# A decoder step on one core: other paces for the decode between two attentions, a query buffer of its own, and POOL loads put behind a norm

## The chip, the cores and the metric

The kernel runs on one core of a Trainium2 chip. The metric is the time of one execution on the device, in microseconds; for the kernel before it is 1862.74 us, the median of 3 runs (1859.68 to 1864.82). One more execution was profiled; all views of the profile come from it.

## What is computed

One step of a one-layer hybrid decoder, for a prompt of 1024 rows (model width 1024) and for 8 sample rows that share the weights. Cut to what matters here:

```python
# the prompt: 1024 rows
q, k, v, logf, u, z = mixer_inputs(rmsnorm(xp, g_mix), w_in, b_f, g_sgu_v)
xp = xp + merge_heads(fox_prompt(q, k, v, logf), sgu_prompt(u, z, w_s, b_s), g_att_out, g_sgu_out, w_o)
mk, mv = memory_kv(mem_prompt, g_mem, w_ck, w_cv)             # 256 memory rows
xp = xp + cross_attend(rmsnorm(xp, g_cross), mk, mv, w_cq, w_co)
xp = xp + conv_ffn(rmsnorm(xp, g_ffn), 0, w_up, conv_w, conv_b, w_down)
# the sample: 8 rows, each with 8192 cached positions in 64 pages
q, k, v, logf, u, z = mixer_inputs(rmsnorm(xs, g_mix), w_in, b_f, g_sgu_v)
att = fox_sample(q, k, v, logf, cache_k, cache_v, cache_logf, page_table)
xs = xs + merge_heads(att, sgu_sample(u, z, w_s, b_s), g_att_out, g_sgu_out, w_o)
xs = xs + cross_attend(rmsnorm(xs, g_cross), cache_mem_k, cache_mem_v, w_cq, w_co)
xs = xs + conv_ffn(rmsnorm(xs, g_ffn), state_conv, w_up, conv_w, conv_b, w_down)
```

`fox_prompt` is causal attention with 8 heads of 64 and a forget gate added to the scores; `fox_sample` is the same for one query row over the paged cache. Both groups are normed once more at the end. All data is float32.

## The kernel before

**Two streams.** `prompt()` and `sample()` are Python generators that emit instructions and yield now and then. The prompt's stream is the main one; the value that it yields is an estimate in microseconds of the TensorE work just emitted. The loop at the end of `build` (L1873 to L1894) adds this value to a credit `acc` and, while the credit has reached a whole pace, takes one advance of the sample's stream; an advance that yields w lowers the credit by w times the pace. After one main yield of t at most `int(t / pace) + 1` advances are taken. The pace is `PACE[phase]` (L76), so a smaller number means a denser sample stream. [...]

**The prompt's stages.** `p1` (L335) makes the input projection: columns for q, for the gates, for k, for v, and for z. Products of float32 data are split in a rounded high part and a rest, three matmuls each (L270 to L272, and L436 to L438 in `by_rows`, which does four blocks of rows at once). Before the last four blocks of z, at `tt == 4`, it calls `early()`, which takes one step of the first attention and one of the fill, and pauses the sample's stream until the first memory product has been emitted. Then come the first attention (rows 0 to 511) mixed one to one with the fill, which is the memory's key and value products (`pmem`, 8 steps of 5.2) and the gating of the first half (`gating`, 8 units); the second attention (rows 512 to 1023) alone; then for each half of the rows the merge, the output projection, the cross-attention (`cross`) and the gated MLP (`ffn`), and a last norm.

**One attention** (`attention`, L686) goes over four pairs of heads `hp`, two blocks of 256 rows each. `load` fetches a pair's rows of q (`qn`, L692), k and v through SyncE's queue. `setup` is a generator in two halves: the first transposes q (L710) and copies it to `qq` (L717 to L734), the second does the same for k (L739 to L752); between them it yields once. `scores` (L755) makes a block of scores (L767 to L771), takes the row maximum on VectorE (L773, or L776 in the second attention) and the exponential on ACT (L774, L777). `turn` transposes the result (L796) and copies it back (L801, L803), `values` multiplies with v (L812), `back` transposes the output (L832) and scales it (L834). Of each pair, eight score blocks yield 1.8 each; while the next pair is being set up, five more yields of 1 follow.

**Buffers.** `T2()` gives one of 7 rotating buffers of 128 x 520 float32, `U()` one of 18 of 4 KB per partition, `KV()` one of 4 of 8 KB per partition, `WRAW()` one of 4 for raw weights. A new use waits until the old one's readers are done. `ssq_into` (L225) takes the sum of squares on ACT and throws the squares into a buffer `junk`.

**The sample's stream.** `decode` (L1316): for each of the 8 rows 16 steps over the cached keys (`kstep`) and, later, 16 over the cached values (`vstep`, eight matmuls L1444 for two steps). `kstep` fetches 1 MB with an indirect DMA from POOL (L1368), then multiplies with q and sums, both on VectorE. In a phase whose name begins with "att" it does this in four pieces (L1375, L1376), each after a yield of 0.2, so that a step of five yields costs one pace; elsewhere in wider instructions (L1384, L1388). `sample_rest` (L1557) follows: output projection, norm, cross-attention, norm, MLP, with their weights and cached memory loaded through POOL's queue into `KV` buffers (L1548, L1607, L1609, L1646, L1700, L1745). Its products with one column block of weights are L284, L1653, L1709 and L1754. `rms8` (L1514) norms the 8 rows: two sums of squares on ACT, a sum and a scale on VectorE (L1520, L221), and the power -0.5 on POOL (L222); `sample_norm` then scales (L1528) and `sample_T` transposes (L309).

**The cross-attention's weights** (`weigh`, L1125): for two blocks of 128 rows at a time the scores (L1135), the negative row maximum on VectorE (L1137), its product with the rows' factor `rq`, on VectorE too (L1138), and the exponential on ACT with that product as bias (L1141).

## Time and profile before

| | |
|---|---|
| median of 3 runs | 1862.74 us |
| profiled execution | 1866.47 us |
| its span, first to last instruction | 1864.6 us |
| instructions | 24289 |
| mean granted TensorE clock | 0.98 |
| HBM traffic | 495.73 MB read, 23.93 MB written, 279 GB/s over the span |
| POOL's software DMA queue | 341.14 MB, 49.0% of 16 DMA engines |
| SyncE's and ACT's hardware DMA queues | 178.58 MB, 27.6% of 16 DMA engines |

How to read the views. PE is TensorE's matmul side and PEld its weight loads, DVE is VectorE, ACT ScalarE, POOL GpSimd, SP SyncE; SPq, POOLq and ACTq are the queues of an engine's sequencer. An instruction stands as line, engine, operation, out<-in by the program's tile names with buffer numbers left out, shapes, and a count. In a timeline the first two columns are the start and the time taken in us, and the brackets hold the idle time of the engine before it and what released it. A row of the waits gives the total in us, how often, and the longest. The slices are 40 equal parts of the span, 46.6 us each; a digit is the busy share in tenths.

### The profile page before, as it was taken

What the parts mean: (1) busy time and instruction counts of PE and PEld (TensorE: products, weight loads), DVE (VectorE), ACT (ScalarE), POOL (GpSimd) and SP (SyncE); (2) the same over time, 40 slices, a digit from 0 to 9 for tenths busy, and PEclk for the clock granted to TensorE, in tenths of its full rate; (3) what the DMA queues carried; (4) which work ended last, traced back from release to release, by engine and by line L of the source; (5) the groups of instructions that cost most, each with busy time, mean ns of one, the idle gap of its engine ahead of it and who ended that gap; (6) DMA issues with size and microseconds to landing.
All of it is one profiled execution on the core that took longest, in us unless ns stands there. A gap on an engine that the chain in (4) does not pass through costs nothing.

```text
span 1864.6 us, 24289 instructions
## 1 busy us (share of the span) xinstructions
PE 1787.5 (96%) x9239; PEld 1299.2 (70%) x9239; DVE 1398.8 (75%) x1736; ACT 735.8 (39%) x1341; POOL 499.3 (27%) x461
## 2 busy tenths in 40 slices
PE   8999999888998999999999999998999999999998
PEld 5887676556676667767777776766676668767765
DVE  4788667888778787989989899898874559644344
ACT  6332364466633535323333234234353333232332
POOL 1243323433142322223242223234322111101110
PEclk9999999899999999999999999999999999999999
DMA  8877886967687975878878789988869577767971
GB/s 316 290 267 265 312 276 239 298 231 230 238 345 287 346 289 209 309 249 328 304 279 319 260 305 344 355 311 329 304 241 349 203 291 259 264 205 260 356 263 59
DMA packets 157012, 521.27 MB, mean 280 GB/s; under 512 B 20808, under 2 KB 40520, under 8 KB 124128
## 3 DMA queue, kind: packets, MB, share of 16 engines
q0 software_dynamic: 57168, 341.14, 49.0%
q1 hardware_dynamic: 92816, 165.99, 25.8%
q10 hardware_dynamic: 6912, 12.59, 1.8%
q8 instruction: 73, 1.20, 0.3%
q14 instruction: 43, 0.35, 0.1%
HBM read 495.73 MB, written 23.93 MB: 279 GB/s over the span
## 4 chain that ended last, share of the span: by engine, by line
PE 59%; DMA 7%; DVE 5%; issue 4%; ACT 2%; POOL 1%; DVEq 0%; POOLq 0%; ACTq 0%
PE ba L270 8%; PE ba L272 8%; PE ba L271 8%; PE bb L270 4%; PE bb L271 4%; PE bb L272 4%; PE dv L1444 4%; DMA kv<-cache_v,kidx 2%; DMA kv<-cache_k,kidx 2%; DVE s L1388 1%; DVE kv L1384 1%; PE dv L1709 1%; PE ba L1021 1%; DMA u<-an_d 1%; PE bb L812 1%
## 5 line engine op out<-in xcount | busy, mean ns | idle before, releaser
L233 ACT ACTIVATE wh<-wr 128x1024 fp32r<-128x1024 f32 (+2 forms) x220 | 228.8, 1044 | 516.6 <-PE ba L271 192.0
L234 DVE TENSOR_TENSOR wl<-wr,wh 128x1024 fp32r<-128x1024 f32 (+2 forms) x220 | 262.9, 1201 | 144.6 <-PE ba L272 62.4
L1368 POOL DMA_INDIRECT kv<-cache_k,kidx x128 | 194.8, 1522 | 569.5 <-DVE s L1388 317.4
L1384 DVE TENSOR_TENSOR kv<-kv,d 128x1024 f32<-128x1024 f32 (+1 forms) x156 | 258.0, 1681 | 29.8 <-DMA kv<-cache_k,kidx 29.5
L1388 DVE TENSOR_REDUCE s<-kv 128x16 f32<-128x1024 f32 (+1 forms) x156 | 258.0, 1673 | 0.0
L1438 POOL DMA_INDIRECT kv<-cache_v,kidx x128 | 159.2, 1244 | 314.7 <-PE dv L1444 244.4
L270 PE MATMUL ba<-u,wh 128*128 128x512 f32 (+1 forms) x560 | 221.3, 397 | 2.0 <-ACT u L236 1.9
L271 PE MATMUL ba<-u,wh 128*128 128x512 f32 (+1 forms) x560 | 221.1, 395 | 1.3 <-DVE u L237 1.2
L272 PE MATMUL ba<-u,wl 128*128 128x512 f32 (+1 forms) x560 | 220.5, 395 | 0.0
L270 PE MATMUL ba<-wh,u 128*128 128x512 f32 (+1 forms) x495 | 187.5, 381 | 0.0
L271 PE MATMUL ba<-wl,u 128*128 128x512 f32 (+1 forms) x495 | 186.5, 378 | 0.0
L272 PE MATMUL ba<-wh,u 128*128 128x512 f32 (+1 forms) x495 | 184.0, 377 | 0.0
L1444 PE MATMUL dv<-kv,s 128*32 128x512 f32 x1024 | 128.1, 603 | 5.0 <-DMA kv<-cache_v,kidx 3.0
L270 PEld LDWEIGHTS ba<-u,wh 128*128 128x128 f32 x560 | 107.0, 191 | 34.6 <-issue 7.2
L272 PEld LDWEIGHTS ba<-u,wl 128*128 128x128 f32 x560 | 107.1, 191 | 32.9 <-issue 9.2
L271 PEld LDWEIGHTS ba<-u,wh 128*128 128x128 f32 x560 | 107.1, 191 | 30.9 <-issue 6.3
L271 PE MATMUL bb<-u,wh 128*128 128x512 f32 (+1 forms) x304 | 118.3, 390 | 8.7 <-DVE u L237 8.7
L270 PE MATMUL bb<-u,wh 128*128 128x512 f32 (+1 forms) x304 | 117.8, 388 | 0.2 <-ACT u L236 0.2
L272 PE MATMUL bb<-u,wl 128*128 128x512 f32 (+1 forms) x304 | 117.1, 386 | 0.0
L270 PEld LDWEIGHTS ba<-wh,u 128*128 128x128 f32 x495 | 93.8, 190 | 27.0 <-issue 8.0
L271 PEld LDWEIGHTS ba<-wl,u 128*128 128x128 f32 x495 | 93.7, 189 | 20.7 <-issue 4.2
L272 PEld LDWEIGHTS ba<-wh,u 128*128 128x128 f32 x495 | 93.5, 189 | 19.7 <-issue 2.5
(437 smaller groups left out, 3293.7 us busy)
## 6 DMA issues: line engine op xcount, KB each, us to landing
wr<-w_up SPq DMA_DIRECT2D x88, 512.0 KB
kv<-w_up POOLq DMA_DIRECT2D x22, 1024.0 KB
wr<-w_down SPq DMA_DIRECT2D x40, 512.0 KB
kv<-w_down POOLq DMA_DIRECT2D x11, 1024.0 KB
wr<-w_in SPq DMA_DIRECT2D x16, 512.0 KB
wr<-w_o SPq DMA_DIRECT2D x16, 512.0 KB
wr<-w_cq SPq DMA_DIRECT2D x16, 512.0 KB
wr<-w_co SPq DMA_DIRECT2D x16, 512.0 KB
```

Source lines behind the costliest of these rows:

```text
L233: nc.scalar.activation(h, src, AF.Copy)
L234: nc.vector.tensor_tensor(l, src, h.bitcast(F32), op=ALU.subtract)
L270: mmul(out, sh, mh, start=(i == 0), stop=False)
L271: mmul(out, sh, ml, start=False, stop=False)
L272: mmul(out, sl, mh, start=False, stop=(i == n - 1))
L812: mmul(po[64 * j : 64 * j + 64, q0:256], vn[:, kt, 64 * j : 64 * j + 64], pt[j][kt // 4][:, kt % 4, q0:256], start=(kt == 0), stop=(kt == ...
L1021: mmul(pss[i], mh[k][:, tb], wh, start=(k == korder[0]), stop=False)
L1368: nc.gpsimd.indirect_dma_start(kv, None, a["cache_k"], off(kidx[:, b, ch : ch + 1]))
L1384: nc.vector.tensor_tensor(kvv[:, i : i + m, :], kvv[:, i : i + m, :], qb.unsqueeze(1).broadcast_to((P, m, 512)), op=ALU.mult)
L1388: nc.vector.tensor_reduce(s[:, ch * 4 + i : ch * 4 + i + m, :].rearrange("p k h -> p (k h)"), kvv[:, i : i + m, :].rearrange("p k (h d) -> ...
L1438: nc.gpsimd.indirect_dma_start(kv, None, a["cache_v"], off(kidx[:, b, ch : ch + 1]))
L1444: mmul(dv[32 * j : 32 * j + 32, :], s[:, ch * 4 : ch * 4 + 4, :].rearrange("p k h -> p (k h)"), kvv[:, j, :], start=(ch == 1), stop=(ch == ...
```

## The change

Five edits:

1. **Paces.** `att0` goes from 16 to 12, `att1` from 10 to 11, and the first attention's pairs 2 and 3 get a phase of their own, `attx`, with 26.
2. **First setup.** In the first attention both halves of pair 0's setup are emitted in the call from `early()`, before the last four blocks of z; before, the second half came as the first step of the mixed stage. The second attention keeps the old form.
3. **Buffers.** `qn` gets one buffer of its own instead of a T2 buffer. To make room, T2 shrinks from 520 to 512 columns, `junk` from 1024 to 512, and sums of squares over more than 512 columns write their squares over their own source (raw rows of x, xs and mem that nothing else reads).
4. **Cross-attention.** The product of the maximum with `rq` moves from VectorE (one instruction for two blocks) to ACT (two copies with a per-row scale).
5. **page.** The loads that `sample_rest` issues through POOL go through `page`, which orders each behind the power of the latest `rms8`.

```diff
-PACE = {'p1': 7.0, 'att0': 16.0, 'mid0': 8.0, 'ffn0': 8.5, 'att1': 10.0, 'mid1': 6.8, 'ffn1': 2.5, 'rest': 2.9}
+PACE = {'p1': 7.0, 'att0': 12.0, 'attx': 26.0, 'mid0': 8.0, 'ffn0': 8.5, 'att1': 11.0, 'mid1': 6.8, 'ffn1': 2.5, 'rest': 2.9}
...
     def T2(n=512, dt=F32):
-        return tpool.tile([P, 520], dt, tag="t2", bufs=NT, name=nm("t2"))[:, :n]
+        return tpool.tile([P, 512], dt, tag="t2", bufs=NT, name=nm("t2"))[:, :n]
...
     def ssq_into(dst, src):
         n = src.shape[-1]
-        j = tpool.tile([P, 1024], BF16, tag="junk", bufs=1, name=nm("junk"))[: src.shape[0], :n]
+
+        j = src if n > 512 else tpool.tile([P, 512], BF16, tag="junk", bufs=1, name=nm("junk"))[: src.shape[0], :n]
         nc.scalar.activation(j, src, AF.Square, accum_out=dst)
...
         def load(hp):
             cs = slice(hp * P, (hp + 1) * P)
-            qn = T2().rearrange("p (i c) -> p i c", c=P)
+            qn = tpool.tile([P, 512], F32, tag="qn", bufs=1, name=nm("qn")).rearrange("p (i c) -> p i c", c=P)
...
         first = setup(0, *load(0))
-        next(first)
-        yield 2
+        if hf:
+            next(first)
+            yield 2
         for _ in first:
             pass
...
             qkv, nxt = got.pop(), None
+            if hf == 0 and hp == 2:
+                phase[0] = "attx"
             for blk in range(2):
...
             mx = sm([P, 4], "cmx", 2)
+            bs = sm([P, 4], "cbs", 2)
...
                 nc.vector.tensor_reduce(mx[:, g2], sv, axis=AX.X, op=ALU.max, negate=True)
-                nc.vector.tensor_tensor(mx[:, g2], mx[:, g2], rq[:, g2], op=ALU.mult)
+                for i2 in range(2):
+                    i = g * 2 + i2
+                    nc.scalar.activation(bs[:, i : i + 1], mx[:, i : i + 1], AF.Copy, scale=rq[:, i : i + 1])
                 for i2 in range(2):
                     i = g * 2 + i2
                     nc.scalar.activation(
-                        pp[h][:, i, :], sv[:, i2, :], AF.Exp, bias=mx[:, i : i + 1], scale=rq[:, i : i + 1], accum_out=l4[:, i : i + 1]
+                        pp[h][:, i, :], sv[:, i2, :], AF.Exp, bias=bs[:, i : i + 1], scale=rq[:, i : i + 1], accum_out=l4[:, i : i + 1]
                     )
...
+    rows8 = []
+
+    def page(dst, src):
+
+        with tc.issue_after(rows8[0]) if rows8 else nullcontext():
+            nc.gpsimd.dma_start(dst, src)
+
     def rms8(src):
...
-        return rstd_of(st, D, 1, "r1")
+        r = rstd_of(st, D, 1, "r1")
+        rows8[:] = [newest(ENG.Pool)]
+        return r
...
-                    nc.gpsimd.dma_start(raw, w[kk * 256 : (kk + 2) * 256, n * 512 : (n + 1) * 512].rearrange("(k p) n -> p k n", p=P))
+                    page(raw, w[kk * 256 : (kk + 2) * 256, n * 512 : (n + 1) * 512].rearrange("(k p) n -> p k n", p=P))
...
-                nc.gpsimd.dma_start(raw.rearrange("p (f d) -> p f d", f=2), a["w_up"][f : f + 2].rearrange("f p d -> p f d"))
+                page(raw.rearrange("p (f d) -> p f d", f=2), a["w_up"][f : f + 2].rearrange("f p d -> p f d"))
```

The loads of q2s_d, cmk, cmv and w_down change to `page` in the same way.

More of the change, by code (lines that the diff above doesn't have):

```diff
@@ L1606, in sample_rest @@
             for n in range(2):
-                nc.gpsimd.dma_start(qb[n], q2s_d[b : b + 1, n * 512 : (n + 1) * 512].broadcast_to((P, 512)))
+                page(qb[n], q2s_d[b : b + 1, n * 512 : (n + 1) * 512].broadcast_to((P, 512)))
             kv = KV()
-            nc.gpsimd.dma_start(kv.rearrange("p (a c) -> p a c", c=D), a["cmk"][b].rearrange("(a p) c -> p a c", p=P))
+            page(kv.rearrange("p (a c) -> p a c", c=D), a["cmk"][b].rearrange("(a p) c -> p a c", p=P))
             kvv = kv.rearrange("p (a c) -> p a c", c=D)
@@ L1645, in sample_rest @@
                 kvs.append(KV().rearrange("p (a c) -> p a c", c=D))
-                nc.gpsimd.dma_start(kvs[-1], a["cmv"][b].rearrange("(a p) c -> p a c", p=P))
+                page(kvs[-1], a["cmv"][b].rearrange("(a p) c -> p a c", p=P))
             for b in (b0 + 1, b0):
@@ L1744, in sample_rest @@
                 raws.append(KV().rearrange("p (f d) -> p f d", f=2))
-                nc.gpsimd.dma_start(raws[-1], a["w_down"][f2 * P : (f2 + 2) * P, :].rearrange("(f p) d -> p f d", p=P))
+                page(raws[-1], a["w_down"][f2 * P : (f2 + 2) * P, :].rearrange("(f p) d -> p f d", p=P))
             yield 1
```

## The prediction

> **What bounds the kernel now.** I read the page first: busy shares, the 40 slices, the chain of waits.

> ```profile
> PE 1787.5 (96%) x9239; PEld 1299.2 (70%) x9239; DVE 1398.8 (75%) x1736; ACT 735.8 (39%) x1341; POOL 499.3 (27%) x461
> PE   8999999888998999999999999998999999999998
> PE 59%; DMA 7%; DVE 5%; issue 4%; ACT 2%; POOL 1%; DVEq 0%; POOLq 0%; ACTq 0%
> ```

> TensorE is busy in all but 77 us of 1864.6. The change removes no product, so all it can win is idle time of TensorE and products that ran at a reduced clock. The digits fall below 9 in a few places, the widest being slices 7 to 9 (326 to 466 us), the two attentions. So I asked next for busy time by stage: the first attention's pairs 0 and 1, which have the memory products beside them, its pairs 2 and 3, and the second attention (the columns are length, busy time with instruction count on PE, PEld, DVE, ACT, POOL, then granted clock, DMA share, GB/s).

> ```profile
> 270.00:335.00 65.00, 60.12 (x317) 43.47 (x316) 46.67 (x77) 33.19 (x71) 23.55 (x31) 0.95 0.74 253
> 335.00:386.00 51.00, 39.57 (x246) 26.51 (x245) 42.81 (x93) 25.43 (x74) 22.83 (x29) 0.87 0.79 259
> 386.00:512.00 126.00, 112.09 (x764) 77.88 (x764) 104.98 (x172) 77.33 (x158) 32.67 (x42) 0.95 0.70 240
> 386.00:400.00 14.00, 9.78 (x56) 6.66 (x56) 11.77 (x21) 9.09 (x23) 0.58 (x1) 0.83 0.64 225
> ```

> Call a stage's loss its idle time plus busy time times (1 - clock). Pairs 0 and 1 lose 4.9 + 3.0 = 7.9 us, pairs 2 and 3 lose 11.4 + 5.1 = 16.5, the second attention 13.9 + 5.6 = 19.5, and its first 14 us alone 4.2 + 1.7 = 5.9. In pairs 2 and 3 VectorE is busy 42.8 of 51 us, more than TensorE. The waits inside that stage, and VectorE's groups by form in both stages (pairs 2 and 3, then 0 and 1), say why:

> ```profile
> PE bb L796 <- ACT t L774: 6.9, 6, 2.3
> ACT t L774 <- DVE mx L773: 12.5, 5, 7.5
> L1376 DVE TENSOR_REDUCE s<-kv 128x8 f32<-128x512 f32 x13 | 8.7, 678 | 0.1
> L1375 DVE TENSOR_TENSOR kv<-kv,d 128x512 f32<-128x512 f32 x12 | 8.7, 734 | 0.0
> ...
> L1375 DVE TENSOR_TENSOR kv<-kv,d 128x512 f32<-128x512 f32 x16 | 10.8, 680 | 0.0
> L1376 DVE TENSOR_REDUCE s<-kv 128x8 f32<-128x512 f32 x16 | 10.4, 681 | 0.1
> ```

> The transposes (L796) wait for the exponentials (L774), these for the row maximum (L773), and the maximum stands in VectorE's queue among decode pieces. One piece is a L1375 and a L1376, 1.4 us together.

> **Paces, last pairs: -5 us.** The emission loop adds the estimated time of each yield to a credit. In an attention one advance of the decode costs 0.2 of the pace and is made only when the credit has reached a whole pace; four advances in five carry a piece. A pair yields 8 x 1.8 units and, while it sets up the next, 5 more: 19.4, the last 14.4 and 2; the fill yields 8 x 5.2 + 8 = 49.6 and runs even with the attention until it ends. So pairs 0 and 1 with their fill yield 4 x 19.4 = 77.6 units, pairs 2 and 3 with the rest of the fill 46.6. Before, 46.6 / 3.2 = 14 advances, 11 pieces (the rows show 12 to 13). After, the credit must first climb from about 12 to 26, and the 32 or 33 units left give 32.6 / 5.2 = 6 advances, 5 pieces. So 7 pieces go, 7 x 1.4 = 9.8 us of VectorE, and its share falls from 0.84 to 0.65, below the 0.72 of pairs 0 and 1. The gain lies between nothing (the chain of score, maximum, exponential, transpose sets the end by itself) and the fall to the loss rate of pairs 0 and 1, 16.5 - 51 x 7.9 / 65 = 10.3. I take half: -5.

> **Paces, first pairs: +2.** 77.6 units at 2.4 instead of 3.2 per advance are 32 instead of 24 (19 pieces; the rows show 16), so 6 or 7 pieces more, +9 us on VectorE: (46.7 + 9) / 65 = 0.86. The cover is the memory products, 60 us of TensorE in the 65. The bounds are nothing and, if the cover failed, the loss rate of the stage with the same VectorE share (386 to 400: 5.9 / 14 = 0.42), 65 x 0.42 - 7.9 = +19.5. With that much product work between the scores I stay near the low end.

> **Paces, second attention: +1.** 74.6 units at 2.2 instead of 2.0 are 34 advances instead of 37. But the phase now starts with a credit near 26 instead of 16, worth (26 - 11) / 2.2 = 7 advances instead of 3: 41 against 40. The sparser pace is eaten, and some 3 pieces move into the first pair, at the stage that loses most. Bounds 0 and 3 pieces x 1.4 = 4; I take 1. No decode is pushed into later phases.

> **First setup and queries: -2.** The key half of pair 0's setup (four transposes, two copies, two casts, two subtractions, four small POOL stores) is now emitted before the last input products, which cover it; the scores then stand ahead of the first memory products instead of behind. What lies there now, on PE and in the SyncE queue:

> ```profile
> 277.01 0.33 PE L796 MATMUL bb<-cp,t 128*128 128x128 f32 x1 [2.36 <-ACT t L774]
> 282.05 1.11 PE L710 MATMUL ba<-cp,t 128*128 128x128 f32 x4 [1.58 <-DMA t<-q_d]
> 282.00:285.00 3.00, 2.95 (x10) 2.45 (x11) 1.33 (x3) 1.61 (x3) 1.13 (x2) 0.50 0.00 0
> 267.47 8.59 SPq L247 DMA_DIRECT2D wr<-w_cv  x4
> 276.11 0.50 SPq L693 DMA_DIRECT2D t<-q_d  x1
> L693 SPq EVENT_SEMAPHORE  x4: 17/4394/12088, 301.1 to 374.7; - x4
> ```

> The one query load that TensorE waited for (1.58) left late because SyncE had w_cv loads ahead of it, not for want of a buffer: the buffer waits (up to 12.1 us) come later, 301 to 375, and no product waited on them. So the new buffer by itself wins little. It has one copy, and its next load waits for transposes that ran a pair earlier. At most 2.36 + 1.58 + 1.5 (the 2.95 at half clock) = 5.4 could go; a late key load inside the input products could cost what the late query load did, 1.6. I take -2. The narrower t2 and the in-place squares change no count of instructions: 0 (ACT, 39% busy, hides them).

> **page: -5.7.** POOL, VectorE and TensorE around the sample's last norm before w_up, and the half clock after it:

> ```profile
> 1660.50 1.57 POOL L1700 DMA_DIRECT2D kv<-w_up  x2 [0.16 <-issue]
> 1677.11 0.71 POOL L1700 DMA_DIRECT2D kv<-w_up  x1 [15.03 <-DMA o_s<-kv]
> 1677.84 0.55 POOL L222 TENSOR_TENSOR r1r<-r1r,mhalf 8x1 f32<-8x1 f32 x1
> ...
> 1669.71 0.14 DVE L221 TENSOR_SCALAR r1r<-sss 8x1 f32<-8x1 f32 x1
> 1678.43 0.87 DVE L1528 TENSOR_SCALAR s<-dec,r1r 8x512 f32<-8x512 f32 x2 [8.58 <-POOL r1r L222]
> ...
> 1678.96 1.02 PE L309 MATMUL ms<-cp,s 8*128 8x8 f32 x8 [3.19 <-DVE s L1528]
> 1675.00:1687.00 12.00, 8.81 (x32) 6.80 (x30) 7.62 (x13) 2.50 (x5) 1.26 (x2) 0.72 0.47 161
> ```

> A fourth w_up load stood 15.03 us on POOL for a buffer, and the power for the norm (0.55 us), ready at 1669.85, stood behind it; TensorE idled 3.19 us, then lost 8.81 x 0.28 = 2.5 at half clock. With the loads ordered behind the power it runs at 1670, L1528 and L309 are ready before 1673, and TensorE reaches L309 at 1675.8 anyway: -5.7.

> [...]

> The price: loads that ran ahead of a norm now wait for it, and behind them on POOL all later loads. For w_cq:

> ```profile
> 1488.79 2.46 POOL L1548 DMA_DIRECT2D kv<-w_cq  x3 [11.49 <-PE dv L284]
> 1499.93 0.56 POOL L222 TENSOR_TENSOR r1r<-r1r,mhalf 8x1 f32<-8x1 f32 x1 [5.73 <-DVE r1r L221]
> 1511.36 1.92 PE L284 MATMUL dv<-kv,xsT 128*32 128x512 f32 x16
> 1504.00:1507.00 3.00, 3.00 (x19) 2.31 (x18) 0.92 (x2) 0.00 (x0) 0.00 (x0) 1.00 0.65 249
> 1507.00:1510.00 3.00, 3.00 (x15) 2.43 (x14) 0.69 (x1) 0.00 (x0) 0.00 (x0) 1.00 0.03 12
> ```

> They leave at 1500.5, 11.7 us later; the transfers that ended by 1507 end by 1519 at worst, and the users stand at 1511. If the products keep their place, TensorE stalls up to 7 us there; if they are placed after the data, prompt products fill in and only the sample's chain is later. That chain has room: it ends with L1777, the prompt's products 18.7 us later.

> ```profile
> 1836.91 1.40 DVE L1777 SCALAR_TENSOR_TENSOR dec<-dec,r1r,d 8x512 f32<-8x512 f32 x2 [0.75 <-POOL r1r L222]
> 1857.00 0.40 PE L272 MATMUL bb<-wh,u 128*128 128x512 f32 x1
> ```

> I take no stall; the other bound is one as dear as the one removed, +5.7.

> **weigh: -2.5.** VectorE, ACT and PE at the dearest place:

> ```profile
> 1297.59 1.28 DVE L1137 TENSOR_REDUCE cmx<-ba 128x2 f32<-128x512 f32 x2
> 1298.79 2.33 DVE L1388 TENSOR_REDUCE s<-kv 128x16 f32<-128x1024 f32 x2
> 1301.05 0.22 DVE L1138 TENSOR_TENSOR cmx<-cmx,rq 128x2 f32<-128x2 f32 x2
> 1301.23 0.56 ACT L1141 ACTIVATE u<-ba,cmx,rq 128x256 f32<-128x256 f32 x1 [3.32 <-DVE cmx L1138]
> 1302.48 3.13 PE L1135 MATMUL ba<-t,u 128*128 128x256 f32 x8 [3.86 <-ACT u L1141]
> L989 ACT ACTIVATE fac<-sqx,part x8: 282/293/297, 702.8 to 1380.0; 128x1 f32<-128x1 f32 x8
> L1248 ACT ACTIVATE hlast<-ba x61: 153/160/165, 740.3 to 1826.7; 128x2 f32<-128x2 f32 x61
> ```

> A product of 0.22 us stood behind 2.33 us of decode. As copies on ACT it follows the maximum directly: the exponentials start near 1298.9 instead of 1301.2, less two more copies at 0.16 to 0.29 (no row has a copy with a pointer as scale; these two are the nearest). The stall falls from 3.86 to about 2.1, and some of the slow clock behind it goes: -2.5, between +1 (the copies, where nothing waited) and -4. The exponentials and splits queued behind the 32 new copies on ACT lose 5 to 9 us in all, at places where ACT waits anyway.

> [...]

> **Sum:** -5 + 2 + 1 - 2 - 5.7 - 2.5 = -12.2. The profiled execution took 1866.47 us (span 1864.6), the median of the runs is 3.73 lower: 1862.74 - 12.2 = 1850.5.

> **Rivals.** *Late loads.* w_cq's products keep their place and stall: page at +5.7 instead of -5.7, sum -0.8, 1862. For it: POOL is in order and the loads leave 11.7 us later. Against it: no sample product waits for its weights now. *VectorE binds the first pairs.* The maxima queue behind the added pieces and the memory products queue behind the transposes in TensorE's order. It decides once VectorE's share there passes the 0.84 of 386 to 400; I expect 0.86. Price: +19.5 instead of +2 in the first pairs, +4 instead of +1 in the second attention, sum +8.3, 1871: slower. For it: L796 stood 2.36 us at 277 with the old pace. Against: 60 us of products in that stage. *The change does not do what it says*: the credit carried over makes the second attention no sparser; that is in the sum.

> **Chances.** Forecast 0.60, its own range 1841 to 1857. Late loads 0.16, VectorE-bound first pairs 0.18, and 0.06 for a larger gain or a mixture. A measurement here tells about 0.3%, 5.6 us, from no change: faster 0.63, same 0.18, slower 0.19. The range reaches from a sum of -24 (upper gains in the last pairs, start and norm together) to just below the slow rival: 1839 to 1869.

> **What would show it.** In the profile after: no wait of L309 on L1528 and no half clock behind it; POOL's power ahead of every w_cq and w_up load; 5 or 6 decode pieces in pairs 2 and 3 and VectorE's share there near 0.65; 22 or 23 pieces in pairs 0 and 1 with TensorE idle not above 7 us; ACT's exponentials in the cross-attention behind L1137, not L1138. The forecast is wrong if pairs 0 and 1 lose over 20 us, if the products on w_cq wait, or if pairs 2 and 3 keep their 11 us of idle with fewer pieces.

## The result and the profile after

The changed kernel takes 1846.57 us (median of 6 runs, 1842.74 to 1850.82), the kernel before 1864.07 us beside it (6 runs, 1859.68 to 1865.58). The ratio is 0.9904, 95% interval 0.9888 to 0.992: about 17.5 us faster. Its profiled execution took 1850.82 us, with a span of 1849.0.

Lines of the code from L226 on have moved down: the scores L767 are L768, the gate's product L609 is L610, the gain row's load L588 is L589, the decode pieces L1375 and L1376 are L1382 and L1383, the value products L1444 are L1451, the row statistic's product L309 is L310.

The page after (busy shares, TensorE's slices, the chain):

```profile
PE 1776.0 (96%) x9239; PEld 1292.5 (70%) x9239; DVE 1396.8 (76%) x1720; ACT 743.0 (40%) x1373; POOL 504.3 (27%) x461
PE   8999999688998999999999999989999999999998
PE 62%; DMA 4%; issue 4%; DVE 3%; ACT 2%; POOL 1%; POOLq 0%; DVEq 0%; ACTq 0%; SPq 0%
```

TensorE's idle time has hardly moved: 1849.0 - 1776.0 = 73 us, before 77. What went is time in which products ran slowly: busy time fell by 11.5 us for the same products. The clock records of the traces say most of the reason. They hold windows with a granted clock of 0.50, each a multiple of 3.41 us but for the last, which the end of the execution cuts off; summed, 75.4 us before and 58.4 after. At 0.50 these 17 us are worth at most 8.5 us of busy time. Some 2 us more went in one group of products (L1444, the cached values: 128.1 us busy before, 125.0 after; the last section says why).

A milestone table says where. It takes from the traces the start of the first product of each stage, in us: the first score, the output projection w_o of the first half, the transposes of the norm behind it (cq0), the first product of w_co (co0), the transposes of the norm before the MLP (ffn0), the same for the second half (ending in ffn1), the sample's value products over the cached memory (pv), the end.

```
              score  w_o0   cq0    co0   ffn0   w_o1    cq1    co1   ffn1     pv     end
before        270.3 507.2 558.6  667.1  720.2 1159.4 1209.1 1320.5 1376.2 1612.2  1864.6
changed       261.6 507.2 558.0  665.8  721.1 1150.8 1198.5 1309.5 1366.0 1602.9  1849.0
```

The scores start 8.7 us earlier, and w_o, behind the two attentions, starts at the same moment as before: the memory products, which stood ahead of the scores, now stand among them. The stretch from ffn0 to w_o1 is 9.5 us shorter (429.7 for 439.2), the stretch from pv to the end 6.3 (246.1 for 252.4). The three stages of the attentions, the first one from 262 us, where it now starts, and from 270 us, then three later windows (columns as in the prediction):

```profile
262.00:326.00 64.00, 62.36 (x347) 45.36 (x346) 52.78 (x86) 38.19 (x80) 26.79 (x33) 1.00 0.83 290
270.00:325.00 55.00, 53.36 (x302) 38.16 (x300) 48.90 (x77) 30.89 (x62) 24.87 (x31) 1.00 0.87 304
325.00:382.00 57.00, 39.68 (x256) 28.92 (x252) 40.50 (x89) 26.20 (x75) 20.37 (x28) 0.88 0.69 239
382.00:508.00 126.00, 111.19 (x746) 75.22 (x745) 101.25 (x170) 74.67 (x155) 32.04 (x42) 0.95 0.66 218
...
555.00:580.00 25.00, 21.48 (x129) 17.89 (x128) 23.72 (x37) 10.25 (x23) 6.42 (x6) 0.86 0.78 302
...
655.00:680.00 25.00, 22.45 (x106) 13.10 (x107) 17.41 (x21) 9.57 (x22) 6.46 (x6) 1.00 0.60 211
...
1110.00:1160.00 50.00, 49.94 (x248) 38.10 (x247) 46.12 (x54) 23.07 (x41) 15.10 (x10) 1.00 0.87 319
```

Pairs 0 and 1 (first two rows) lose 1.6 us, 7.9 before. Pairs 2 and 3 lose 17.3 idle and 4.8 at half clock, 22.1 after 16.5: worse, although they hold 9 decode pieces, where 326 to 382 us held 14 before (in the prediction's own window, 335 to 386 us, 5 instead of 12 or 13). The second attention loses 14.8 + 5.6 = 20.4, before 19.5. In the changed kernel's waits a new row stands first, and the wait of L310 on the row statistic is gone from the list:

```profile
PE ba L610 <- DVE u L602: 11.1, 1, 11.1
PE bb L272 <- DVE u L238: 9.0, 3, 5.1
```

The timeline of the changed kernel, rows of several engines in order of time: the new wait at 350.77, one cross-attention at 1282, the two norms of the sample at 1489 and 1660:

```profile
330.64 4.13 SPq L599 DMA_DIRECT2D u<-zg_d  x1
...
334.38 0.34 ACTq L682 DMA_DIRECT2D o_mv<-t  x1
...
334.87 5.15 SPq L600 DMA_DIRECT2D u<-sgu_d  x1
340.12 1.42 SPq L589 DMA_DIRECT2D t<-g_sgu_v  x1
...
349.30 2.74 DVE L602 SCALAR_TENSOR_TENSOR u<-u,rz,t 128x512 f32<-128x512 f32 x4 [10.44 <-DMA t<-g_sgu_v]
350.77 3.78 PE L610 MATMUL ba<-u,u 128*128 128x128 f32 x16 [11.09 <-DVE u L602]
...
657.09 1.92 PE L1451 MATMUL dv<-kv,s 128*32 128x512 f32 x16 [2.37 <-DMA kv<-cache_v,kidx]
...
1282.98 1.27 DVE L1142 TENSOR_REDUCE cmx<-ba 128x2 f32<-128x512 f32 x2
1284.18 2.32 DVE L1395 TENSOR_REDUCE s<-kv 128x16 f32<-128x1024 f32 x2
1284.66 0.46 ACT L1145 ACTIVATE cbs<-cmx,rq 128x1 f32<-128x1 f32 x2
1285.03 0.55 ACT L1148 ACTIVATE u<-ba,cbs,rq 128x256 f32<-128x256 f32 x1
...
1489.85 0.54 POOL L222 TENSOR_TENSOR r1r<-r1r,mhalf 8x1 f32<-8x1 f32 x1 [22.64 <-DVE r1r L221]
1490.35 2.45 POOL L1526 DMA_DIRECT2D kv<-w_cq  x3
1501.27 1.06 PE L285 MATMUL dv<-kv,xsT 128*32 128x512 f32 x8
...
1660.80 0.55 POOL L222 TENSOR_TENSOR r1r<-r1r,mhalf 8x1 f32<-8x1 f32 x1 [35.40 <-DVE r1r L221]
1661.32 2.87 POOL L1526 DMA_DIRECT2D kv<-w_up  x4
1666.50 0.66 PE L310 MATMUL ms<-cp,s 8*128 8x8 f32 x8
```

The gate multiplies its rows with a gain row (g_sgu_v) that it loads into a T2 buffer. That load (L589) stands last among the gate's loads in SyncE's queue, at 340.12; VectorE waits 10.44 us for it, and TensorE 11.09 us behind VectorE. That its buffer is one that a store of the memory values (L682, 334.38) had just read fits the times, and is not shown. The load is issued at 340.12 and used at 349.30, so most of the wait is the load itself on its way. A load of 0.25 MB (128 x 512 float32) so holds up TensorE.

At 1283 the copy on ACT follows the maximum directly, while the decode's sum (L1395, 2.32 us), behind which its product used to stand, runs beside it. At 1489 and 1660 the power now stands ahead of the loads; the w_cq products at 1501 and L310 at 1666 have no wait in brackets.

### The profile page after: what moved, and what is told of

Its sections match the earlier page's. It is cut to its first block, busy times and chain, and to the rows that moved or that the text cites. A ratio compares the mean times of both kernels' runs of the same rounds, so it can differ in the third digit from the quotient of the medians.

```text
span 1849.0 us, 24314 instructions
## 1 busy us (share of the span) xinstructions
PE 1776.0 (96%) x9239; PEld 1292.5 (70%) x9239; DVE 1396.8 (76%) x1720; ACT 743.0 (40%) x1373; POOL 504.3 (27%) x461
## 4 chain that ended last, share of the span: by engine, by line
PE 62%; DMA 4%; issue 4%; DVE 3%; ACT 2%; POOL 1%; POOLq 0%; DVEq 0%; ACTq 0%; SPq 0%
PE ba L271 9%; PE ba L272 9%; PE ba L273 9%; PE bb L271 5%; PE bb L272 5%; PE bb L273 5%; PE dv L1451 4%; DMA kv<-cache_k,kidx 2%; PE dv L1725 1%; PE ba L1025 1%; PE ba L1026 1%; PE ba L1027 1%; DMA kv<-cache_v,kidx 1%; DVE s L1395 1%; POOL kv L1375 1%
## 5 line engine op out<-in xcount | busy, mean ns | idle before, releaser
L1375 POOL DMA_INDIRECT kv<-cache_k,kidx x128 | 202.8, 1584 | 549.3 <-DVE s L1395 296.6
L1391 DVE TENSOR_TENSOR kv<-kv,d 128x1024 f32<-128x1024 f32 (+1 forms) x156 | 257.8, 1680 | 31.1 <-DMA kv<-cache_k,kidx 22.3
L1395 DVE TENSOR_REDUCE s<-kv 128x16 f32<-128x1024 f32 (+1 forms) x156 | 258.1, 1672 | 0.0
L272 PE MATMUL ba<-u,wh 128*128 128x512 f32 (+1 forms) x560 | 219.9, 393 | 2.0 <-DVE u L238 1.9
L272 PE MATMUL ba<-wl,u 128*128 128x512 f32 (+1 forms) x495 | 186.0, 376 | 0.3 <-DVE wl L235 0.2
L1451 PE MATMUL dv<-kv,s 128*32 128x512 f32 x1024 | 125.0, 598 | 4.1 <-DMA kv<-cache_v,kidx 4.1
L272 PE MATMUL bb<-u,wh 128*128 128x512 f32 (+1 forms) x304 | 119.4, 393 | 9.0 <-DVE u L238 9.0
L272 PEld LDWEIGHTS ba<-u,wh 128*128 128x128 f32 x560 | 106.5, 190 | 29.8 <-issue 4.6
L272 PEld LDWEIGHTS ba<-wl,u 128*128 128x128 f32 x495 | 93.0, 188 | 22.5 <-issue 5.5
```

The source lines that it names most:

```text
L272: mmul(out, sh, ml, start=False, stop=False)
L1375: nc.gpsimd.indirect_dma_start(kv, None, a["cache_k"], off(kidx[:, b, ch : ch + 1]))
L1391: nc.vector.tensor_tensor(kvv[:, i : i + m, :], kvv[:, i : i + m, :], qb.unsqueeze(1).broadcast_to((P, m, 512)), op=ALU.mult)
L1395: nc.vector.tensor_reduce(s[:, ch * 4 + i : ch * 4 + i + m, :].rearrange("p k h -> p (k h)"), kvv[:, i : i + m, :].rearrange("p k (h d) -> ...
L1451: mmul(dv[32 * j : 32 * j + 32, :], s[:, ch * 4 : ch * 4 + 4, :].rearrange("p k h -> p (k h)"), kvv[:, j, :], start=(ch == 1), stop=(ch == ...
```

## The experiments

**What was open.** The trace shows three gains (the stretch ffn0 to w_o1, the stretch after pv, the start) and a loss that the forecast had not seen (the gain row). My theory was that the page edit takes its stall away, the set-up brings the start, the paces the rest, and that the late gain row hides part of it. The rival: the edits are not separable, since each moves, everywhere behind it, the order in which a planner of the compiler framework puts the instructions. All runs are compared with the kernel before on the same chip: its medians were 1864.21 (first group), 1863.3, 1864.1 and 1865.27 us. The changed kernel was run in the first comparison only, so differences to it are between medians of different groups; taken from the ratios instead they come out 1 to 3 us larger or smaller (the set-up undone costs 14 us by the ratios instead of 11.5, the early gain row wins 6 instead of 7.5), and each is uncertain by some 4 us.

**Each edit alone.** The page edit on the kernel before:

```diff
-                nc.gpsimd.dma_start(...)
+                page(...)
```

> Only edit 5 (page) on the kernel before. Theory: the norm's power no longer stands behind the fourth w_up load, the stall of 3.19 us on L309 and the half clock behind it go: 5.7 to 6.4 us less, ratio 0.9967, and no wait of the w_cq products on their weights. Rival (late loads): the loads held back to the norm make the products on w_cq wait, ratio 0.999 to 1.003.

1861.25 us, ratio 0.9982 (0.9964 to 1.0001). In its trace the stretch after pv is 246.0 us, as in the changed kernel, against 252.4 before: the stall is gone, while the interval of the time reaches from the forecast to no change. What the edit is worth depends on its company: with the paces alone (below), without this edit, the wait of L309 on L1528 is only 0.6 us, and that stretch 239.8 us. The weighing alone:

```diff
-                nc.vector.tensor_tensor(mx[:, g2], mx[:, g2], rq[:, g2], op=ALU.mult)
+                for i2 in range(2):
+                    i = g * 2 + i2
+                    nc.scalar.activation(bs[:, i : i + 1], mx[:, i : i + 1], AF.Copy, scale=rq[:, i : i + 1])
```

> Only edit 4 (the product with rq on ACT) on the kernel before. Theory: the wait of the scores of the second cross-attention on the exponentials (3.86 us) shrinks, 2.5 us less, ratio 0.9987, with nothing lost in the first cross-attention. Rival: the copies stand behind other work on ACT and the first cross-attention gives back 2 to 3 us, ratio 1.000. Second rival: the planner's new order moves stalls elsewhere by more than either, ratio away from 1 by over 0.003.

1865.5 us, ratio 0.9999 (0.9979 to 1.0019): no difference. In the milestones below the second cross-attention (cq1 to co1) is 3.7 us shorter than before (107.7 for 111.4) and the first (cq0 to co0) 5.0 us longer (113.5 for 108.5), as the first rival said. One trace does not show that the edit does both: in the other traces with the old weighing the second stretch is 110 to 120 us, in those with the new one 105 to 115. The paces alone:

```diff
-PACE = {'p1': 7.0, 'att0': 16.0, 'mid0': 8.0, 'ffn0': 8.5, 'att1': 10.0, ...
+PACE = {'p1': 7.0, 'att0': 12.0, 'attx': 26.0, 'mid0': 8.0, 'ffn0': 8.5, 'att1': 11.0, ...
```

> Only edit 1 (paces and attx) on the kernel before. Theory of the prediction: pairs 2 and 3 lose about 5 us less, pairs 0 and 1 about 2 more, the second attention 1 more: 2 us less, ratio 0.999. Rival: the last pairs are set by the gating's loads and the chain of the scores, not by the decode's pieces; then they keep their 16 us of loss, ratio 1.000 to 1.003. Second rival: it is the denser decode that brought the 11 us wait on the gain row of the gate in the changed kernel; then this kernel shows that wait too, ratio 1.004 or more.

1865.75 us, ratio 1.0008 (0.9991 to 1.0024). That is the first rival: pairs 2 and 3 keep their loss (10.9 us idle and 17.7 lost from 326 to 382 us, before 11.1 and 16.5) with 7 or 8 decode pieces instead of 12 or 13 in the prediction's window. The second rival falls, since the gate's products wait far less here than in the changed kernel:

```profile
PE ba L609 <- DVE u L601: 3.2, 1, 3.2
PE bb L609 <- DVE u L601: 2.0, 1, 2.0
```

The first set-up, the queries' buffer and the two buffer sizes:

```diff
-        next(first)
-        yield 2
+        if hf:
+            next(first)
+            yield 2
...
-            qn = T2().rearrange("p (i c) -> p i c", c=P)
+            qn = tpool.tile([P, 512], F32, tag="qn", ...
```

> Only edits 2 and 3 (whole first setup in early, query buffer, narrower t2) on the kernel before. Theory: the start of the first attention loses about 7 us less, as it does in the changed kernel, because the first scores stand ahead of the memory products; ratio 0.996 if nothing else moves. Rival: the late gain row (a wait of some 11 us of the gating's products) comes with these two edits, because the memory products end later beside the attention; then ratio 0.999 to 1.003 and the wait is seen here.

1860.93 us, ratio 0.9983 (0.9965 to 1.0001). The gain row's load is the last of the gate's here (342.3 us), as its rival said, but the gate's products wait 0.7 us and not 11. The four together would make 0.18 + 0.01 - 0.08 + 0.17 = 0.28%, about 5 us; measured at once they make 0.96%. The four intervals are each 0.2% wide to either side, and some 0.4% for their sum, so the difference is clear of the noise: the edits do not add. Their milestones:

```
              score  w_o0   cq0    co0   ffn0   w_o1    cq1    co1   ffn1     pv     end
page          270.4 507.3 559.6  667.9  721.0 1159.4 1209.1 1320.2 1375.9 1612.7  1858.7
weighing      269.6 507.0 559.5  673.0  724.5 1165.4 1212.5 1320.2 1375.6 1613.0  1863.6
paces         270.2 519.2 569.1  677.5  732.7 1162.4 1211.7 1331.5 1385.8 1626.6  1866.4
set-up        261.8 507.3 558.8  668.2  719.7 1154.3 1204.0 1314.5 1367.9 1605.3  1859.2
```

Alone, the paces cost 12 us in the attentions (519.2) and win 9.5 in the stretch ffn0 to w_o1 (429.7 for 439.2).

**Each edit undone in the changed kernel.** First the set-up with both buffers:

```diff
-        if hf:
-            next(first)
-            yield 2
+        next(first)
+        yield 2
...
-            qn = tpool.tile([P, 512], F32, tag="qn", ...
+            qn = T2().rearrange("p (i c) -> p i c", c=P)
```

> The changed kernel with the first set-up, the queries' buffer and the two buffer sizes of before (paces, page and weighing stay changed). The edits measured singly came to about -3 us together, all of them at once to -17.5. Theory 'the pair': the paces cost about 12 us in the two attentions as long as the first set-up is the old one (first product of w_o at 519.2 us with the new paces alone, 507.2 before) and nothing once it is the new one; then this kernel's first product of w_o comes at about 519 us, its stretch from there to the up-projection's first half stays short, and its median is 1855 to 1862. Rival 'sum': each edit brings the same wherever it is made; then undoing this one costs the 3 us that it brought alone, median 1849 to 1851, first product of w_o at 507 to 510 us. By both the 11.1 us wait of the gate's product on the gain row goes, since that row's load stands ahead of the gate's other loads in SyncE's queue again.

1858.05 us, ratio 0.998 (0.9963 to 0.9997), w_o0 at 518.3: the theory of the pair holds. The edit that brought 3 us alone is worth 11.5 us here. The paces undone:

```diff
-PACE = {'p1': 7.0, 'att0': 12.0, 'attx': 26.0, 'mid0': 8.0, 'ffn0': 8.5, 'att1': 11.0, ...
+PACE = {'p1': 7.0, 'att0': 16.0, 'mid0': 8.0, 'ffn0': 8.5, 'att1': 10.0, ...
...
-            if hf == 0 and hp == 2:
-                phase[0] = "attx"
```

> The changed kernel with the paces of before (16 and 10, no separate pace for the last pairs); the other four edits stay. Theory 'the pair': in the traces the stretch of the first up and down projections (first up-projection to the second half's w_o) lasts 429.8 us in the changed kernel and with the new paces alone, against 439.2 before, 438.4 with the page alone and 434.6 with the set-up alone; so the paces' gain lies there, in the waits of L901 and L1444 that are gone, and this kernel gets them back: median 1851 to 1856, that stretch 434 to 440 us, attentions as in the changed kernel within 2 us. Rival 'the paces act in the first attention', as the prediction had it: the stretch stays near 430 us and the last pairs of the first attention change instead; the wait of the gate's product on the gain row, if the paces made it, is gone. Theory: that wait stays, since with the set-up and queries' buffer alone the row's load is already the last in the queue.

1852.14 us, ratio 0.994 (0.9926 to 0.9954), 5.6 us slower than the changed kernel. w_o starts at 506.5 (507.2), the stretch ffn0 to w_o1 is back at 436.5. The spans of the two traces are 1847.6 and 1849.0 us, the other way round, so they cannot show where the 5.6 us of the medians lie. This kernel's longest wait between 1100 and 1160 us (L903 is the merge's transpose):

```profile
PE ba L903 <- DMA u<-an_d: 2.4, 2, 1.5
```

Its longest wait from 262 to 330 us:

```profile
PE ms L813 <- ACT u L804: 5.6, 1, 5.6
```

The windows:

```profile
262.00:326.00 64.00, 55.71 (x295) 40.47 (x293) 41.46 (x67) 34.78 (x72) 18.12 (x25) 0.95 0.65 225
...
1110.00:1160.00 50.00, 46.49 (x229) 32.09 (x228) 47.51 (x57) 24.09 (x41) 14.55 (x12) 0.97 0.94 345
```

Its loads for the gate:

```profile
323.05 0.34 SPq L591 DMA_DIRECT2D u<-wsT  x1
...
341.96 0.35 SPq L589 DMA_DIRECT2D t<-g_sgu_v  x1
```

At 1110 to 1160 us, where the merge of the second half begins, TensorE idles 3.5 us with the old paces and 0.06 with the new (row above). And in 262 to 326 us it idles 8.3 us, 5.6 of them in one wait on a copy by ACT (L804); with the early set-up and the denser pace that wait is gone. The gain row's load is last here too, so the paces did not put it there. But the wait behind it is gone: L610 waits 0.6 us, where my theory had said that the wait stays. So the 11.1 us take both edits. The gate's products run at nearly the same time in both kernels (349.4 us here, 350.8 in the changed one); as I read it, with the dense pace TensorE has done its other work by then and stands idle.

The page edit undone:

```diff
-        with tc.issue_after(rows8[0]) if rows8 else nullcontext():
-            nc.gpsimd.dma_start(dst, src)
+        nc.gpsimd.dma_start(dst, src)
```

> The changed kernel with the single-row work's loads issued as before (no order on GpSimd's queue against the row statistics). Theory: TensorE waits about 3 us at L310 on the row statistic again, with 3 to 7 us of half clock behind it; the stretch from the value products to the end goes from 246.1 us back to 250 to 253; median 1850 to 1853 (+3 to +6.4). Rival 'the other edits had already moved that wait out' (with the new paces alone the stretch lasted 239.8 us without this edit): no wait at L310, stretch within 1 us of 246.1, median 1846 to 1848.

1850.68 us, ratio 0.9932 (0.9918 to 0.9945), 4.1 us slower; the stretch from pv (1603.5 us) to the end is 1854.7 - 1603.5 = 251.2 us. The stall is back in its waits:

```profile
PE ms L310 <- DVE s L1544: 3.1, 1, 3.1
```

The set-up undone but the queries' buffer kept:

```diff
-        if hf:
-            next(first)
-            yield 2
+        next(first)
+        yield 2
```

> The changed kernel with the first set-up alone as before (it runs inside the paced steps again); the queries keep their own buffer, and paces, page and weighing stay changed. It splits what undoing both cost (1858.05 us, first product of w_o at 518.3 us). Theory 'the early set-up frees the first pairs': the first score comes at about 270 us again instead of 261.6, the attentions end at 515 to 520 us, median 1853 to 1859. Rival 'the buffer': it is the rotation of the shared buffers that the queries no longer take part in; then the attentions end at 506 to 509 us as in the changed kernel, the median is 1845 to 1850, and the gain row's load is still the last of the gate's in SyncE's queue.

1862.31 us, ratio 0.9983 (0.9971 to 0.9995). The score starts at 271.4, w_o0 at 513.9, a little better than expected, but the median is 3 us above the theory's range: the loss goes on behind the attentions (w_o0 to ffn0 219.4 us, 213.9 in the changed kernel). The rival falls. The gate's loads in this kernel's queue:

```profile
331.20 0.34 SPq L589 DMA_DIRECT2D t<-g_sgu_v  x1
331.71 0.34 SPq L591 DMA_DIRECT2D u<-wsT  x1
```

The gain row is first again although the queries still have their own buffer. In the changed kernel, with the set-up and buffers alone, and with the paces undone, it is the last; in both kernels where the set-up was undone, with the queries' buffer or without, the first. So the early set-up, not the queries' buffer, is what puts it last; I read it as the rotation of the T2 buffers standing elsewhere when the gate asks for one. The weighing undone:

```diff
-                for i2 in range(2):
-                    i = g * 2 + i2
-                    nc.scalar.activation(bs[:, i : i + 1], mx[:, i : i + 1], AF.Copy, scale=rq[:, i : i + 1])
+                nc.vector.tensor_tensor(mx[:, g2], mx[:, g2], rq[:, g2], op=ALU.mult)
```

> The changed kernel with the negated maximum times its row factor on VectorE in one instruction again, instead of two copies on ScalarE; the rest stays. Alone this edit measured 1865.5 against 1864.2 us, which is no difference. Theory 'nothing to see': within 0.2% of the changed kernel, 1843 to 1850. Rival of the prediction (the edit brings 2.5 us in the two cross-attentions): 1848 to 1852, and the waits of TensorE on the exponentials at L1140 and L1168 are 2 us longer together.

1849.24 us, ratio 0.9911 (0.9895 to 0.9927) against 0.9904 (0.9888 to 0.992): the intervals lie on each other, and 1849.24 is in both theories' ranges. Undecided; if the edit is worth anything it is about 1 to 3 us. In the trace the second cross-attention is again longer without the edit (117.2 us for 111.0) and the first shorter (105.4 for 107.8); the signs are those of the weighing alone, and the same caution holds.

**The second attention's pace alone.** The pace that the forecast had priced at 1 us was taken back by itself:

```diff
-'att0': 12.0, 'attx': 26.0, ..., 'att1': 11.0
+'att0': 12.0, 'attx': 26.0, ..., 'att1': 10.0
```

> The changed kernel with the second attention's pace at 10 as before; the first attention keeps 12 and then 26. All four traces with the new paces have a stretch of 429.4 to 430.8 us from the first half's up-projection to the second half's w_o, all four with the old ones 434.6 to 440.9. Theory 'the shift': any change of the number of pieces that are done before that stretch moves its pieces against the waits of L901 and L1444; with pace 10 in the second attention the pieces ahead are one fewer or more and the stretch is 434 us or longer, median 1849 to 1854. Rival 'the first attention's paces do it': the stretch stays at 429 to 431 us, median 1844 to 1849.

1865.42 us, ratio 0.9995 (0.998 to 1.0011): 19 us slower than the changed kernel. Neither theory had this. The stretch ffn0 to w_o1 stayed short (429.0), as the rival said, and the time is far from both. Of the 14.1 us between the two spans, 3.8 have come by w_o0; from cq0 to co0 14.9 more come (122.7 us for 107.8), and behind pv 7.6 are won back (238.5 for 246.1). Its waits in the first cross-attention, 558 to 700 us, and VectorE's queue ahead of them (L977 is the residual addition, L238 a split, L1391 and L1395 are decode pieces):

```profile
PE bb L272 <- DVE u L238: 6.5, 2, 4.0
PE ba L1076 <- DVE u L977: 3.8, 2, 2.7
PE ba L1140 <- ACT t L1127: 2.9, 1, 2.9
```

```profile
559.20 2.35 DVE L1391 TENSOR_TENSOR kv<-kv,d 128x1024 f32<-128x1024 f32 x2
561.47 1.22 DVE L235 TENSOR_TENSOR wl<-wr,wh 128x1024 fp32r<-128x1024 f32 x1
562.60 2.34 DVE L1395 TENSOR_REDUCE s<-kv 128x16 f32<-128x1024 f32 x2
564.86 2.35 DVE L1391 TENSOR_TENSOR kv<-kv,d 128x1024 f32<-128x1024 f32 x2
567.12 0.69 DVE L977 TENSOR_TENSOR u<-ba,u 128x512 f32<-128x512 f32 x1
```

Here 7 us of decode stand ahead of the last residual additions, on which the norm of the whole half waits. In the changed kernel these places hold one wait of 3.5 us. To see if that is the cause, the decode was held one step earlier at this norm, pace 10 kept:

```diff
                     if len(group) == 2 and k == korder[3]:
+                        held[0] = phase[0] == "mid0" and ys is None
                         yield 5.2
```

> The kernel with the second attention's pace back at 10 (1865.42 us), with one difference: in the first half's w_o the decode is held one step earlier, so that the decode piece that stood in VectorE's queue ahead of the last two residual additions (L977) is issued after the norm. In the trace of the 1865 us kernel TensorE waits 2.7 and 1.1 us there on L977 and then 2.5 and 4.0 us on the splits (L272 on L238), with 17 us of half clock between 571 and 605 us; the changed kernel has one such wait of 3.5 us. The stretch from w_o's end (first transpose of the norm) to the first product of w_co is 122.7 us in the one and 107.8 in the other. Theory 'place': what decides is which decode piece stands ahead of this norm, and the second attention's pace only moves it; then the waits on L977 go and the stretch falls to 107 to 115 us, median 1850 to 1858. Rival 'amount': the denser pace costs its work wherever it stands; the waits move to the next pieces, the stretch stays at 118 to 124 us, median 1861 to 1867.

1863.27 us, ratio 0.9989 (0.9974 to 1.0003). The theory's local part holds: the stretch cq0 to co0 falls from 122.7 to 113.1 us, and the waits there are small now:

```profile
PE ba L610 <- issue: 2.3, 1, 2.3
PE bb L1141 <- ACT t L1128: 2.2, 1, 2.2
PE ba L1077 <- DVE u L977: 1.5, 2, 1.1
```

(Lines behind the added one stand one further in this kernel.) The median went by the rival. Of the 9.4 us that are won by w_o1 most are given back in the second cross-attention and its w_co:

```
                    score  w_o0   cq0    co0   ffn0   w_o1    cq1    co1   ffn1     pv     end
pace 10             261.8 511.0 563.6  686.3  737.5 1166.5 1217.3 1328.1 1385.0 1624.6  1863.1
pace 10, held       263.1 511.3 563.8  676.9  728.1 1157.1 1207.9 1322.7 1382.5 1622.0  1861.2
```

From cq1 to co1 it is 114.8 us instead of 110.8, from co1 to ffn1 59.8 instead of 56.9. So the place of a decode piece at a norm is worth some 10 us there, and that is shown; of these 10 us only 2 reach the end, and what makes the pace worth 19 us at the end is not settled.

**The gain row early.** The one loss with a name was taken out: the gain row of the first half goes into one of the decode's row buffers, which is free long before.

```diff
-        gsv = T2()
+        gsv = D2() if hf == 0 else T2()
```

> The changed kernel with the gate's gain row of the first half in one of the five decode row buffers, so that its load need not wait for a store of the memory values and is issued ahead. Theory: the 11.1 us wait of TensorE at L610 ends within 3 us, with most of the 13.7 us of half clock behind it: idle minus 8 to 11 us and clock minus 4 to 7 us in the stretch 325 to 382 us; what of it reaches the end depends on whether another wait follows: median 1834 to 1842. Rival 'the attentions end at 507 us anyway' (the first product of w_o came at 507.0 to 507.3 us in five of six traces, with this wait and without it): the stall is gone but the second attention waits that much longer on ScalarE's exponentials or on VectorE's decode pieces, first product of w_o at 505 to 508 us, median 1844 to 1849. A decode buffer short: pieces of the decode wait for a row buffer, slower than 1849.

1839.03 us (4 runs, 1837.06 to 1840.87), ratio 0.9873 (0.9857 to 0.9888): the fastest kernel here, 7.5 us below the changed one. The load, its waits, and the windows:

```profile
139.25 0.36 SPq L589 DMA_DIRECT2D d<-g_sgu_v  x1
...
345.84 1.42 DVE L602 SCALAR_TENSOR_TENSOR u<-u,rz,d 128x512 f32<-128x512 f32 x2 [2.30 <-DMA u<-zg_d]
347.31 1.67 PE L610 MATMUL bb<-u,u 128*128 128x128 f32 x8 [4.76 <-DVE u L602]
```

```profile
262.00:326.00 64.00, 62.72 (x350) 45.80 (x349) 53.02 (x86) 38.07 (x81) 25.91 (x33) 1.00 0.83 298
326.00:382.00 56.00, 43.82 (x283) 32.58 (x283) 44.33 (x97) 30.26 (x85) 21.16 (x30) 0.94 0.75 251
```

The 11.1 us are gone; 4.8 of them come back behind the second load of z rows (zg_d), more than the 3 expected, so the gain is less than the stall. w_o starts at 499.1 us, which ends the rival's picture of a fixed end at 507 us.

## Why the prediction was right, and where its terms were not

The forecast was 1850.5 us, measured are 1846.57: direction, size and interval came out, but not for all its reasons. The losses of TensorE in the attentions (idle time plus busy time times one less the clock) put the terms apart. Each entry is the range over the traces with this set-up and these paces; the kernel of the early gain row and the two with pace 10 in the second attention are left out.

```
                                              262 to 326   326 to 382   382 to 508 us
old set-up, old paces (before, page, weighing)  5.3-7.6     16.5-18.6    19.4-20.4
old set-up, new paces (3 traces)                6.0-6.7     16.4-17.7    25.0-28.8
new set-up, old paces (2 traces)               10.3-11.1    19.8         12.7-12.8
new set-up, new paces (changed, and 2 more)     1.3-4.0     19.8-22.0    18.5-21.9
```

**The page term (-5.7) had the right mechanism.** The power runs ahead of the loads, the wait of L309 (now L310) is gone, and the late w_cq loads cost nothing: they leave at 1490.35, right behind the power, and their product at 1501 waits for none. In the traces the stretch behind pv gets 6.3 us shorter; in the medians the edit is worth 3 us alone and 4.1 undone. The term was read from one execution whose stall was followed by two half-clock windows (6.8 us at 0.50); by the medians it is a little smaller. *Late loads* as a rival falls.

**Weighing (-2.5): mechanism seen, size not.** The exponentials follow the maximum as forecast (1282.98 and 1284.66), one copy takes 281 ns (32 of them, median), inside the 160 to 290 that were assumed, and TensorE's wait of 3.86 us on the exponentials is gone from the second cross-attention. A wait of 2.4 us on the next copies by ACT (L1168 on L1161) stands there instead, and 3.4 us at a clock of 0.50 follow in both kernels (from 1303.2 us before, from 1301.1 in the changed one). In time the edit is 0 alone and within the noise undone; neither a gain nor a cost of the copies is shown.

**Last pairs (-5): the step that failed.** The counting was right: in the prediction's own windows the changed kernel has 22 to 24 and 5 decode pieces, where 22 or 23 and 5 or 6 were forecast, and VectorE's share in pairs 2 and 3 is 32.74 / 51 = 0.64. The step from VectorE's share to TensorE's idle time was wrong. The wait that the term names, the transposes on the exponentials, did shrink with the pieces: from 335 to 386 us it is 6.9 us before, 3.1 with the paces alone and 1.0 in the changed kernel. But the gate's products, which waited 0.6 us there before, now wait 5.2 with the paces alone and 11.1 in the changed kernel, and the idle time did not fall in any kernel with the new paces: 11.4 us before, 12.2 to 18.0 in the others. That is the forecast's own sign of being wrong (fewer pieces, the same 11 us of idle). What the changed kernel has above the others is the gain row's. The forecast had treated the buffers as free of cost ("the new buffer by itself wins little"), and did not follow what the moved set-up does to the order of the gate's loads. With the row early, 326 to 382 us loses 12.2 + 43.82 x 0.06 = 14.8, at best 2 us less than before and not 5.

**First pairs (+2) had the wrong sign.** With the old set-up the denser pace changes nothing there that stands out of the traces' spread; with the new set-up it takes the loss from some 11 us to 1 to 4. *VectorE binds the first pairs* falls: VectorE's share there is 48.90 of 55 in the row from 270 us, even above the 0.86 expected (52.78 of 64 from 262 us), and TensorE idles less than ever. It falls without the early set-up too: with the paces alone that share is 53.35 / 65 = 0.82 in the prediction's window, and the loss 6.6 us after 7.9. The 12 us by which w_o comes later with the paces alone do not arise in the first pairs.

**Second attention (+1) was too small.** The changed kernel loses 20.4 us there after 19.5, which looks like the term. But by the table the new paces cost 5 to 9 us there with either set-up, and the early set-up wins about 7; the near agreement is the difference of two effects that the forecast did not have. Why fewer pieces go with more loss there is not settled. The pace of this attention has a condition besides: at 10 the kernel is 19 us slower, mostly by losses behind the attention.

**First set-up and queries (-2): too small, and in the wrong place.** Alone it makes the first pairs lose more and the second attention less. The start gains 8.7 us and gives them back by 507 us; the edit is worth 3 us alone and 11.5 with the others.

**The form of the sum.** Terms were added as if each edit had a price. Alone they make 5 us, at once 17.5; undone one at a time (4.1 + 2.7 + 5.6 + 11.5) they make 24, with an uncertainty too large to tell that from 17.5. That the sum of -12.2 lay near is in good part luck: the last pairs lost where a gain was expected, and the stretch ffn0 to w_o1, where the new paces win 7 to 9.5 us, 3.5 of them idle time at the second half's merge, was in no term.

**What stays open.** Which of the many moved pieces makes pace 11 worth 19 us over pace 10; why the new paces cost the second attention 5 to 9 us; whether the weighing brings anything; and the second wait on z rows in the fastest kernel, which was not tried.

## What to carry to other kernels

When an edit takes a tile out of a rotating pool or moves a step ahead, list who gets the next buffers of that pool: a load of 0.25 MB that stood last of the gate's loads in SyncE's queue held TensorE for 11.1 us here, and 0.6 us with the old paces, as I read it because TensorE got there with other work still to do. Where a planner orders two streams, price edits in pairs and undo them one at a time in the finished kernel, since the same edit was worth 3 us alone and 11.5 in company. Look for decode work queued ahead of serial places (a norm, a merge) as well as at its density, and measure to the end: moving one piece won 10 us at a norm here and 2 in all.

## What the hardware showed unexpectedly

**A broken group of products took extra rounds.** The 1024 products of the cached values, in the changed kernel and then with pace 10:

```profile
L1451 PE MATMUL dv<-kv,s 128*32 128x512 f32 x1024 | 125.0, 598 | 4.1 <-DMA kv<-cache_v,kidx 4.1
```

```profile
L1451 PE MATMUL dv<-kv,s 128*32 128x512 f32 x1024 | 131.5, 605 | 1.0 <-DMA kv<-cache_v,kidx 1.0
```

Two pieces of one group in the timeline with pace 10:

```profile
505.43 1.05 PE L1451 MATMUL dv<-kv,s 128*32 128x512 f32 x4
...
507.57 1.05 PE L1451 MATMUL dv<-kv,s 128*32 128x512 f32 x2
```

At full clock one product takes the same in both, 598 ns on average. A group of 16 takes 1.92 us (657.09 above): in the trace it starts in four rounds, some 430 ns apart, of four products each within 20 ns. With pace 10 prompt products stand inside a group near 505 us and cut it into 10, 4 and 2; these take 1.90, 1.05 and 1.05 us, 4.0 together, since the 16 now start in eight rounds of one to four products, and a round that is not full takes as long (in the changed kernel ten products from 1360.74 us start in rounds of 4, 4, 1 and 1, 430 to 450 ns apart). Counting what each uninterrupted run of these products takes above 0.12 us per product (1.92 / 16), broken groups cost 3.4 us in the changed kernel and 7.2 with pace 10, where two whole groups at half clock cost 1.6 more. That is 5.4 of the 6.5 us between the two rows.
